# Attention with weights times values as three rounded products, row maxima from 64 rows, and reciprocals in four pieces

## The chip, the cores and the metric

The kernel runs as one program on 1 core of one Trainium2 chip. The metric is the device time of an execution in microseconds (us); lower is better. Matmul durations in the profile are modelled from their start, so consecutive matmul rows overlap; what a matmul costs is read from the distance between starts.

## The reference

One layer of a bidirectional encoder is applied with the same weights to two sequences, x_prompt (2048 tokens) and x_sample (256 tokens), all in float32 with a model width of 1024:

```python
h = rmsnorm(x, norm1_w)
p = h @ w_in                                    # 4*512 mLSTM columns, 32 gates, 512 q, 2*128 k and v
m_out = mlstm_mixer(mq, mk, mv, mo, gates, ...) # 8 heads of 64, both directions
a_out = attention_mixer(aq, ak, av, q_norm_w, k_norm_w)
x = x + concat([m_out, a_out]) @ w_out
h = rmsnorm(x, norm2_w)
a, g = split(centred_dwconv(h @ w_up, conv_w, conv_b))
x = x + (silu(g) * a) @ w_down                  # d_ff = 2816
y = rmsnorm(x, final_norm_w)
```

The attention part has 8 query heads and 2 key/value heads of 64 elements. For each group of four heads:

```python
s = einsum('bqhgd,bkhd->bhgqk', qi, k) * 64 ** -0.5
p = softmax(s, axis=-1)
o = einsum('bhgqk,bkhd->bqhgd', p, v)
```

q and k are RMS-normed per head and rotated by position; their norm weights are drawn 8 times larger than usual, so the scores are large and the softmax is sharp.

## The kernel before

A matmul here takes a stationary operand of at most 128 rows (the contraction) by 128 columns and streams a moving operand of at most 512 columns past it. Most products are written as three products of rounded parts: a float32 value x is split into a high part of type F32R (a copy through that type, made on ACT) and a low part x minus high (made on DVE, which writes F32R too); high*high + high*low + low*high is summed in PSUM. F32R operands go through the array in one pass of the matmul instruction. Plain F32 operands are turned into two matmul instructions each.

The program has these stages. `phase_a` projects q, k, v and the gates of every 128-token tile (18 tiles: 16 of the prompt, 2 of the sample), norms and rotates q and k, and stores the high and low parts of q and k (`q_d`, `k_d`) and v (`v_d`) in DRAM. `gate_math` works out the mLSTM gates. Then `run_both` interleaves two generators, `attention` and `mlstm`, by estimates of their cost that they yield; when mLSTM is through, `phase_c` (the product with w_out, tile `po`) follows beside what is left of attention. `phase_d` is the feed-forward part. The code is recorded in this order with priorities, and a scheduler of the tile framework then sets the order of the instructions on each engine from its own model of time. Each engine runs its list in that order.

Attention handles 36 pieces, each of 512 queries (tile names carry head and block): 32 of the prompt, with 16 key tiles of 128 keys, and 4 of the sample, with 2 key tiles. That makes 520 key tiles in all. Per piece:

- `prep` (L488 on) transposes the stored q into `qq` (rows 0 to 63 are q's high part, rows 64 to 127 its low part, 512 queries wide) and `qm` (high part alone, 65 rows; row 64 takes the negated maxima).
- `maxstep` (L512 to L517) takes 128 queries against 512 keys. The stationary operand is `qq`, all 128 rows, the moving one is `kk`, which holds the high part of k twice; DVE reduces the 512 scores of each query to a maximum. A prompt piece has 16 such steps, each one matmul `px` and one reduction `mx`. They belong to the piece after the current one.
- `prep2` (L519 on) reduces the maxima, negates them, and brings them as a row into `qm`.
- `scores` (L532 to L542), for two key tiles at a time: two matmuls per key tile into a PSUM tile `ps` (L539: k high with q high and low; L540: k low and a row of ones with q high and the row of negated maxima), then an exponential on ACT (L541) into the SBUF tile `pe`. With the maxima inside the product, `pe` is already exp(s - max).
- `values` (L544 to L552), two steps of the loop later (`PLAG` = 2): the product of `vv` and `pe` in F32, one for each key tile, added up in the PSUM tile `pv`. `vv` has 64 columns of v and 64 of ones, so rows 64 to 127 of `pv` get the sum of the weights.
- `fin1` (L554 on) copies both halves of `pv` out; `fin2` (L563 on) takes one reciprocal of 64x512 on DVE (L564), multiplies on POOL and stores by a DMA on POOL's queue.

PSUM tiles named `ps`, `px`, `pq` and `pr` share four banks (`SCB` = 4). `load_kv` loads kk, kl and vv for a group of heads in four parts by DMAs on POOL's queue.

Of the kernel before, what the change touches and what calls it, by code (L numbers as in the profile page):

```python
# [17 lines left out]
P = 128  # L18
# [52 lines left out]
PB = 4  # L71
PEB = 5
PLAG = 2
# [12 lines left out]
def f32(ap):  # L86
    return ap.bitcast(F32)
# [50 lines left out]
def phase_a(g, tc, sw, st_x, after_x, after_mm, after_pj):  # L138
# [3 lines left out]
    with ExitStack() as st:  # L142
# [284 lines left out]
def attention(g, tc, s1, s2, pp):  # L427
# [12 lines left out]
    def load_kv(grp, k0, k1, after=None):  # L440

        if (grp, k0) in kv:
            return
        n = k1 - k0
        sp = s2 if n == NT1 else s1
        kv[(grp, k0)] = parts = []
        for t0 in range(0, n, 4):
            m = min(4, n - t0)
            s = f"{n}_{t0}"
            kk = sp.tile([P, m * P], F32R, tag="kk" + s, name=f"kk{grp}_{s}", bufs=1)  # L450
            kl1 = sp.tile([65, m * P], F32R, tag="kl1" + s, name=f"kl1{grp}_{s}", bufs=1)
            vv = sp.tile([P, m, P], F32, tag="vv" + s, name=f"vv{grp}_{s}", bufs=1)
            c = slice((k0 + t0) * P, (k0 + t0 + m) * P)
            if after is not None:
                for t in (kk[0:1, 0:1], kk[HD:HD + 1, 0:1], kl1[0:1, 0:1], vv[0:1, 0, 0:1]):
                    nc.gpsimd.tensor_copy(t, after[0:1, 0:1])
            nc.gpsimd.memset(vv[:, :, HD:P], 1.0)
# [30 lines left out]
    def prep(n):  # L488
# [15 lines left out]
        nc.scalar.activation(s.qq[:, 0:s.N], f32(pq[:, 0:s.N]), AF.Copy)  # L504
        s.qm = sp.tile([65, 512], F32R, tag="qm", name="qm" + s.nm, bufs=2)
        nc.scalar.activation(s.qm[0:HD, 0:s.N], f32(pq[0:HD, 0:s.N]), AF.Copy)
        s.mx = sp.tile([P, 4, 4], F32, tag="mx", name="mx" + s.nm, bufs=2)
        s.nsp = -(-s.nk * P // 512)
        s.todo = [(t, z) for z in range(s.nsp) for t in range(s.nq)]
        return s  # L510

    def maxstep(s):  # L512
        t, z0 = s.todo.pop(0)
        w = min(512, s.nk * P - z0 * 512)
        ps = pp.tile([P, 512], F32, tag="sc", name=f"px{s.nm}_{t}_{z0}")
        nc.tensor.matmul(ps[:, 0:w], s.qq[:, t * P:(t + 1) * P], s.kv[z0][0][:, 0:w], start=True, stop=True)  # L516
        nc.vector.tensor_reduce(s.mx[:, t, z0:z0 + 1], ps[:, 0:w], AX.X, ALU.max)  # L517

# [13 lines left out]
    def scores(s, kp):  # L532
        N = s.N
        pe = sp.tile([P, 2, 512], F32, tag="pe", name=f"pe{s.nm}_{kp}", bufs=PEB)
        for z in range(2):
            ps = pp.tile([P, 512], F32, tag="sc", name=f"ps{s.nm}_{kp}_{z}")
            kk, kl1, _ = s.kv[kp // 2]
            kc = (2 * kp + z) % 4 * P
            nc.tensor.matmul(ps[:, 0:N], kk[:, kc:kc + P], s.qq[:, 0:N], start=True, stop=False)  # L539
            nc.tensor.matmul(ps[:, 0:N], kl1[:, kc:kc + P], s.qm[:, 0:N], start=False, stop=True)  # L540
            nc.scalar.activation(pe[:, z, 0:N], ps[:, 0:N], AF.Exp)  # L541
        return kp, pe  # L542

    def values(s, kp, pe):  # L544

        N = s.N
        if kp == 0:
            s.pv = pp.tile([P, 512], F32, tag="pv", name="pv" + s.nm, bufs=1)
        for z in range(2):
            kt = 2 * kp + z  # L550
            nc.tensor.matmul(s.pv[:, 0:N], s.kv[kp // 2][2][:, kt % 4, :], pe[:, z, 0:N], start=(kt == 0),  # L551
                             stop=(kt == s.nk - 1))  # L552

# [8 lines left out]
    def fin2(s):  # L562
        N = s.N  # L563
        nc.vector.reciprocal(s.rs[:, 0:N], s.rs[:, 0:N])  # L564
        nc.gpsimd.tensor_tensor(s.o1[:, 0:N], s.o1[:, 0:N], s.rs[:, 0:N], ALU.mult)
# [8 lines left out]
    while cur.todo:  # L574
        maxstep(cur)
        yield 0.5
    prep2(cur)
    load_kv(0, 0, NT1, cur.m4)
    old = None
    for n in range(len(hbs)):  # L580
# [3 lines left out]
        for kp in range(nkp):  # L584
# [3 lines left out]
            if nxt is not None and nxt.todo:  # L588
                if n == len(hbs) // 2 - 1:

                    k = 2 * (kp - 2) - (nxt.nq * nxt.nsp - len(nxt.todo))
                else:
                    k = -(-len(nxt.todo) // max(nkp - kp - MXE, 1))
# [648 lines left out]
def body(tc, aps, phases="abcd"):  # L1242
# [5 lines left out]
    with ExitStack() as st:  # L1248
# [6 lines left out]
        def dram(name, shape):  # L1255
            setattr(g, name, dp.tile(shape, F32, name=name))
# [6 lines left out]
        dram("k_d", [2, P, T])  # L1263
        dram("v_d", [2, P, NT, HD])
        dram("nm_d", [NT, 16, P])
# [157 lines left out]
```

## Time and profile before

| | us |
|---|---|
| three runs | 3505.19, 3510.44, 3514.43 |
| median of the runs | 3510.44 |
| profiled execution, span from first to last instruction | 3509.1 |
| first 270 us (phase_a): PE busy / DVE busy | 229.9 / 199.9 |
| 270 to 1812 us (attention beside mLSTM, then beside phase_c): PE / DVE / ACT busy | 1524.8 / 791.8 / 705.6 of 1542 |
| 1812 us to the end: PE / DVE busy | 1652.1 / 1354.2 of 1697.1 |

The profiled execution is listed with its span alone; it is 1.3 us below the median of the runs. The first `pv` matmul starts at 271.8 us, the last at 1812.0 us. In the profile PE is the matmul itself, PEld the loading of its stationary operand; DVE, ACT and POOL are the vector, scalar and general-purpose engines. In a row of groups, "x520 | 292.7, 595" means 520 instructions that kept the engine busy for 292.7 us together, 595 ns each in the mean; behind the second bar stands how long the engine was idle just before them and what ended that. In a row of the timeline the first number is the start in us, the second the time from the first start to the last end of the instructions merged into the row.

### The profile page before, as it was taken

Reading aid. Unit: us, or ns where it says so; the run is one execution under the profiler, and the core shown is the slowest. Engines: PE = TensorE matmul, PEld = TensorE weight load, DVE = VectorE, ACT = ScalarE, POOL = GpSimd, SP = SyncE. Lnnn points to the kernel's source line nnn. Section 1 sums busy time; section 2 is a strip of 40 time slices with the busy share of each in tenths; the row PEclk is TensorE's granted clock in tenths of the full one; section 3 lists DMA queues with packets and bytes.
Section 4 is the critical chain, followed back from the end, with each engine's and each line's share of the span. In section 5 each row is a group of like instructions: output and inputs, shape, how many; then the busy total and the mean of one; then the engine's idle time right before and its main releaser. Section 6 shows DMA issues by size and latency. Waiting matters only on the chain.

```text
span 3509.1 us, 53243 instructions
## 1 busy us (share of the span) xinstructions
PE 3406.8 (97%) x19538; PEld 3031.7 (86%) x19538; DVE 2345.9 (67%) x3962; ACT 1683.3 (48%) x3827; POOL 1144.3 (33%) x1362
## 2 busy tenths in 40 slices
PE   7889999999999999999999999999999999999998
PEld 6787787777777777767789999999999999999998
DVE  7773365546544555664444887878888879887777
ACT  5434454444444454453332544445544445655555
POOL 7863022213231322311135333224433224422222
PEclk9999999999999999999999999999999999999999
DMA  7765233233243434442247323213323213312211
GB/s 234 209 188 147 89 107 100 92 108 106 84 123 111 137 114 133 126 147 80 88 147 252 125 97 103 73 67 123 137 98 108 73 67 123 135 64 73 73 67 54
DMA packets 288917, 401.76 MB, mean 114 GB/s; under 512 B 27408, under 2 KB 188976, under 8 KB 288656
## 3 DMA queue, kind: packets, MB, share of 16 engines
q1 hardware_dynamic: 256560, 355.87, 30.9%
q0 software_dynamic: 10640, 31.86, 3.2%
q10 hardware_dynamic: 21456, 10.62, 1.0%
q8 instruction: 154, 2.52, 0.3%
q14 instruction: 107, 0.88, 0.1%
HBM read 315.55 MB, written 82.72 MB: 113 GB/s over the span
## 4 chain that ended last, share of the span: by engine, by line
PE 75%; DVE 9%; issue 5%; POOL 4%; DMA 4%; ACT 3%; SPq 0%; POOLq 0%; DVEq 0%; ACTq 0%
PE pa L1034 12%; PE pv L551 11%; PE pd L1172 11%; PE pc L1034 6%; PE po L918 5%; PE mv L668 4%; PE mj L658 4%; PE ps L539 3%; PE ps L540 3%; PE px L516 3%; PE pb L1034 3%; PE mN L794 1%; PE mj L684 1%; DVE acc L1174 1%; DVE y L1128 1%
## 5 line engine op out<-in xcount | busy, mean ns | idle before, releaser
L1172 PE MATMUL pd<-act,wd 128*128 128x384 f32 (+1 forms) x3120 | 592.0, 336 | 19.2 <-DVE acc L1174 10.8
L1172 PEld LDWEIGHTS pd<-act,wd 128*128 128x128 f32 x3120 | 540.0, 188 | 26.0 <-DVE acc L1174 14.5
L551 PE MATMUL pv<-pe,vv 128*128 128x512 f32 x1040 | 514.4, 593 | 0.2
L517 DVE TENSOR_REDUCE mx<-px 128x1 f32<-128x512 f32 (+1 forms) x528 | 342.8, 673 | 196.6 <-PE px L516 194.9
L1034 PE MATMUL pa<-nt,wut 128*128 128x386 f32 (+2 forms) x2376 | 454.7, 339 | 2.2 <-ACT u L1050 2.2
L1034 PEld LDWEIGHTS pa<-nt,wut 128*128 128x128 f32 x2376 | 422.2, 190 | 2.5 <-ACT u L1050 2.5
L541 ACT ACTIVATE pe<-ps 128x512 f32<-128x512 f32 x520 | 292.7, 595 | 266.2 <-PE ps L540 262.4
L1039 POOL TENSOR_TENSOR tw<-ru 128x512 f32<-128x512 f32 x66 | 102.1, 1547 | 740.3 <-DMA ru<-w_up 598.6
L1128 DVE SCALAR_TENSOR_TENSOR y<-u,cw,y 128x768 f32<-128x768 f32 (+1 forms) x264 | 308.9, 1171 | 35.8 <-ACT y L1121 28.8
L1174 DVE TENSOR_TENSOR acc<-pd,acc 128x384 f32<-128x384 f32 (+1 forms) x544 | 281.5, 538 | 40.1 <-PE pd L1172 38.1
L1050 ACT ACTIVATE u<-pa 128x386 f32<-128x386 f32 (+2 forms) x264 | 128.8, 488 | 328.3 <-PE pa L1034 325.8
L551 PEld LDWEIGHTS pv<-pe,vv 128*128 128x128 f32 x1040 | 189.0, 189 | 82.8 <-issue 58.3
L539 PE MATMUL ps<-qq,kk 128*128 128x512 f32 x520 | 249.5, 483 | 0.9 <-ACT pe L541 0.6
L918 PE MATMUL po<-cmx,wo 128*128 128x256 f32 x1728 | 242.5, 291 | 1.6 <-DVE wo L107 1.6
L918 PEld LDWEIGHTS po<-cmx,wo 128*128 128x128 f32 x1728 | 222.3, 191 | 24.7 <-issue 17.1
L516 PE MATMUL px<-kk,qq 128*128 128x512 f32 (+1 forms) x528 | 224.5, 455 | 2.7 <-ACT pe L541 1.3
L658 PE MATMUL mj<-mn,wm 128*128 128x256 f32 x1296 | 213.2, 305 | 8.6 <-ACT og L672 4.6
L658 PEld LDWEIGHTS mj<-mn,wm 128*128 128x128 f32 x1296 | 181.8, 194 | 38.0 <-issue 21.1
L540 PE MATMUL ps<-qm,kl 65*128 65x512 f32 x520 | 207.4, 402 | 0.1
L668 PE MATMUL mv<-wm,mn 128*128 128x256 f32 x1296 | 205.0, 298 | 0.4 <-ACT qb L664 0.4
L668 PEld LDWEIGHTS mv<-wm,mn 128*128 128x128 f32 x1296 | 178.1, 192 | 21.6 <-issue 13.9
L226 PE MATMUL pj<-w_a,n1T 128*128 128x512 f32 (+1 forms) x864 | 180.2, 363 | 8.6 <-DVE n1T L184 6.0
(285 smaller groups left out, 6663.8 us busy)
## 6 DMA issues: line engine op xcount, KB each, us to landing
ru<-w_up SPq DMA_DIRECT2D x132, 512.0 KB, 3.2
mn<-n_d SPq DMA_DIRECT2D x216, 256.0 KB, 3.3
rd<-w_down SPq DMA_DIRECT2D x66, 512.0 KB, 3.3
n_d<-n1T SPq DMA_DIRECT2D x18, 1024.0 KB, 5.2
dm<-nm_d POOLq DMA_DIRECT2D x72, 256.0 KB, 3.6
mjn<-n_d SPq DMA_DIRECT2D x72, 256.0 KB, 2.9
mvn<-n_d SPq DMA_DIRECT2D x72, 256.0 KB, 3.2
q_d<-qz SPq DMA_DIRECT2D x18, 512.0 KB, 5.6
```

The source lines that it names most:

```text
L516: nc.tensor.matmul(ps[:, 0:w], s.qq[:, t * P:(t + 1) * P], s.kv[z0][0][:, 0:w], start=True, stop=True)
L517: nc.vector.tensor_reduce(s.mx[:, t, z0:z0 + 1], ps[:, 0:w], AX.X, ALU.max)
L539: nc.tensor.matmul(ps[:, 0:N], kk[:, kc:kc + P], s.qq[:, 0:N], start=True, stop=False)
L540: nc.tensor.matmul(ps[:, 0:N], kl1[:, kc:kc + P], s.qm[:, 0:N], start=False, stop=True)
L551: nc.tensor.matmul(s.pv[:, 0:N], s.kv[kp // 2][2][:, kt % 4, :], pe[:, z, 0:N], start=(kt == 0), stop=(kt == s.nk - 1))
L658: nc.tensor.matmul(pj[:, o], s.w[c][:, a, o * P:(o + 1) * P], nT[c][:, h, :], start=(c + o + k == 0), stop=(c == NCC - 1 and k == 2 and o ...
L668: nc.tensor.matmul(pv[:, o], nT[c][:, a, o * P:(o + 1) * P], s.w[c][:, h, 256:512], start=(c + o + k == 0), stop=(c == NCC - 1 and k == 2 ...
L918: nc.tensor.matmul(po[:, o], wo[c][z // 2][:, a, n], mx[c][:, h, :], start=(c == 0 and k == 0), stop=(c == NCC - 1 and k == 2))
L1034: nc.tensor.matmul(p, w[:, aa, c, :], ops[k][:, c, bb, 0:n], start=c == 0 and i == 0 and not add, stop=c == NCC // 2 - 1 and i == 2, skip_ ...
L1128: nc.vector.scalar_tensor_tensor(y[:, s:e], u[:, s + k:e + k], cw[:, k, jj:jj + 1], y[:, s:e], ALU.mult, ALU.add)
L1172: nc.tensor.matmul(po, wds[j][c // 4][:, aa, c % 4 * P:(c % 4 + 1) * P], acts[j][:, bb, z0:z1], start=(j == 0 and k == 0), stop=(j == len( ...
L1174: nc.vector.tensor_tensor(accs[c][:, z0:z1], po, accs[c][:, z0:z1], ALU.add)
```

## The change

- **Values.** After the exponential, ACT copies `pe` to F32R (high part) and DVE subtracts it from `pe` (low part); both go into an SBUF tile `xx`. `phase_a` splits v in the same way and stores both parts; `load_kv` loads v's high part into `vv` (now F32R) and its low part into a new tile `vl` with 64 columns. For each key tile there are three F32R products into `pv`: vv with the high part, vl with the high part (only rows 0 to 63 of `pv`), vv with the low part.
- **Maxima.** `maxstep` takes q's high part alone: stationary operands of 64 rows, one half of the queries from rows 0 to 63 of `qm`, the other from rows 64 to 127, where `prep` now puts a second copy of q's high part. Two steps are issued together, one in each half of the rows, into two PSUM tiles; then the two reductions. The maxima are those of k high times q high.
- **Reciprocals.** The reciprocal of 64x512 becomes four of 64x128.
- `PEB` goes from 5 tiles of 2x512 to 3 of 512; `XB` = 6 tiles of 2x512 hold the two parts.

```diff
-PEB = 5
+PEB = 3
+XB = 6
...
         def post1(i, pj):
...
-            v = sp.tile([P, 2, HD], F32, tag="v", name=f"v{i}", bufs=2)
-            nc.scalar.activation(v, pj[:, 640:768].rearrange("p (h d) -> p h d", d=HD), AF.Copy)
-            nc.scalar.dma_start(g.v_d[:, :, i, :].rearrange("g p d -> p g d"), v)
+            v = sp.tile([P, 2, 2, HD], F32R, tag="v", name=f"v{i}", bufs=2)
+            pv = pj[:, 640:768].rearrange("p (h d) -> p h d", d=HD)
+            nc.scalar.activation(v[:, :, 0], pv, AF.Copy)
+            nc.vector.tensor_tensor(v[:, :, 1], pv, f32(v[:, :, 0]), ALU.subtract)
+            nc.scalar.dma_start(g.v_d[:, :, i].rearrange("g p a d -> p g a d"), f32(v))
...
-            vv = sp.tile([P, m, P], F32, tag="vv" + s, name=f"vv{grp}_{s}", bufs=1)
+            vv = sp.tile([P, m, P], F32R, tag="vv" + s, name=f"vv{grp}_{s}", bufs=1)
+            vl = sp.tile([P, m, HD], F32R, tag="vl" + s, name=f"vl{grp}_{s}", bufs=1)
...
-            nc.gpsimd.dma_start(vv[:, :, 0:HD], g.v_d[grp, :, k0 + t0:k0 + t0 + m])
-            parts.append((kk, kl1, vv))
+            for a, t in ((0, vv[:, :, 0:HD]), (1, vl)):
+                nc.gpsimd.dma_start(f32(t), g.v_d[grp, :, k0 + t0:k0 + t0 + m, a])
+            parts.append((kk, kl1, vv, vl))
...
-        s.qm = sp.tile([65, 512], F32R, tag="qm", name="qm" + s.nm, bufs=2)
-        nc.scalar.activation(s.qm[0:HD, 0:s.N], f32(pq[0:HD, 0:s.N]), AF.Copy)
+        s.qm = sp.tile([P, 512], F32R, tag="qm", name="qm" + s.nm, bufs=2)
+        for r in (0, HD):
+            nc.scalar.activation(s.qm[r:r + HD, 0:s.N], f32(pq[0:HD, 0:s.N]), AF.Copy)
...
-        s.todo = [(t, z) for z in range(s.nsp) for t in range(s.nq)]
+        s.todo = [(t, z) for z in range(s.nsp) for t in range(0, s.nq, 2)]
...
-        ps = pp.tile([P, 512], F32, tag="sc", name=f"px{s.nm}_{t}_{z0}")
-        nc.tensor.matmul(ps[:, 0:w], s.qq[:, t * P:(t + 1) * P], s.kv[z0][0][:, 0:w], start=True, stop=True)
-        nc.vector.tensor_reduce(s.mx[:, t, z0:z0 + 1], ps[:, 0:w], AX.X, ALU.max)
+        pxs = [pp.tile([P, 512], F32, tag="sc", name=f"px{s.nm}_{t0 + i}_{z0}") for i in range(2)]
+        for i in range(2):
+            r, c = slice(HD * i, HD * i + HD), slice((t0 + i) * P, (t0 + i + 1) * P)
+            nc.tensor.matmul(pxs[i][:, 0:w], s.qm[r, c], s.kv[z0][0][r, 0:w], start=True, stop=True)
+        for i in range(2):
+            nc.vector.tensor_reduce(s.mx[:, t0 + i, z0:z0 + 1], pxs[i][:, 0:w], AX.X, ALU.max)
...
-            nc.tensor.matmul(ps[:, 0:N], kl1[:, kc:kc + P], s.qm[:, 0:N], start=False, stop=True)
-            nc.scalar.activation(pe[:, z, 0:N], ps[:, 0:N], AF.Exp)
+            nc.tensor.matmul(ps[:, 0:N], kl1[:, kc:kc + P], s.qm[0:HD + 1, 0:N], start=False, stop=True)
+            pe = sp.tile([P, 512], F32, tag="pe", name=f"pe{s.nm}_{kp}_{z}", bufs=PEB)
+            x = sp.tile([P, 2, 512], F32R, tag="px", name=f"xx{s.nm}_{kp}_{z}", bufs=XB)
+            nc.scalar.activation(pe[:, 0:N], ps[:, 0:N], AF.Exp)
+            nc.scalar.activation(x[:, 0, 0:N], pe[:, 0:N], AF.Copy)
+            nc.vector.tensor_tensor(x[:, 1, 0:N], pe[:, 0:N], f32(x[:, 0, 0:N]), ALU.subtract)
...
-        for z in range(2):
+        vv, vl = s.kv[kp // 2][2:4]
+        for z, x in enumerate(xs):
             kt = 2 * kp + z
-            nc.tensor.matmul(s.pv[:, 0:N], s.kv[kp // 2][2][:, kt % 4, :], pe[:, z, 0:N], start=(kt == 0),
-                             stop=(kt == s.nk - 1))
+            nc.tensor.matmul(s.pv[:, 0:N], vv[:, kt % 4, :], x[:, 0, 0:N], start=kt == 0, stop=False)
+            nc.tensor.matmul(s.pv[0:HD, 0:N], vl[:, kt % 4, :], x[:, 0, 0:N], start=False, stop=False)
+            nc.tensor.matmul(s.pv[:, 0:N], vv[:, kt % 4, :], x[:, 1, 0:N], start=False, stop=kt == s.nk - 1)
...
-        nc.vector.reciprocal(s.rs[:, 0:N], s.rs[:, 0:N])
+        for t in range(s.nq):
+            c = slice(t * P, (t + 1) * P)
+            nc.vector.reciprocal(s.rs[:, c], s.rs[:, c])
```

The scheduler takes the two maxima matmuls of a step apart in most cases. On PE, before, in a prompt piece of head 4 beside the mLSTM projection `mv` (px is a maxima matmul, ps scores, pv values; 128x512 is the result):

```order
L668 MATMUL mv_0_5189<-wm_6_4792,mn_0_6_5124 128x256 x2
L516 MATMUL px_4_0_1_4711<-kk_16_4_2657,qq_4_4676 128x512
L668 MATMUL mv_0_5189<-wm_6_4792,mn_0_6_5124 128x256 x3
L516 MATMUL px_4_1_1_4714<-kk_16_4_2657,qq_4_4676 128x512
L551 MATMUL pv_4_4894<-pe_4_1_4702,vv_16_0_2646 128x512
L794 MATMUL mN_3_5306<-va_1_2478,dm_3_5051 128x65 x4
L776 MATMUL mS_4_5327<-qb_2_2480,mkT_2_2479 128x256
L516 MATMUL px_4_2_1_4717<-kk_16_4_2657,qq_4_4676 128x512
```

On PE after the change, in a piece of the same head beside the projection `mj` (L524 is the maxima matmul now, with 64 rows; L566, L567 and L568 are the three value products):

```order
L568 MATMUL pv_4_5920<-xx_4_7_0_6289,vv_16_12_2715 128x512
L524 MATMUL px_4_0_0_6352<-kk_16_0_2665,qm_4_6332 128x512
L676 MATMUL mj_3_6872<-mn_3_3_6859,wm_3_5232 128x256 x4
L524 MATMUL px_4_1_0_6353<-kk_16_0_2665,qm_4_6332 128x512
L676 MATMUL mj_3_6872<-mn_3_3_6859,wm_3_5232 128x256
L676 MATMUL mj_3_6872<-mn_3_4_6860,wm_4_5233 128x256
L524 MATMUL px_4_2_0_6358<-kk_16_0_2665,qm_4_6332 128x512
L676 MATMUL mj_3_6872<-mn_3_4_6860,wm_4_5233 128x256 x4
L566 MATMUL pv_4_5920<-xx_4_7_1_6297,vv_16_12_2715 128x512
L755 MATMUL mu_3_7164<-va_1_5292,kw_3_6573 128x130
L567 MATMUL pv_4_5920<-xx_4_7_1_6297,vl_16_12_2716 64x512
```

In both, maxima matmuls stand singly between full-height matmuls; the 64-row ones now do so with another height than their neighbours. Over the whole program the 528 maxima matmuls of the changed kernel stand in 414 stretches without another matmul between: 327 of one, 65 of two, 17 of three and 5 of four. The 520 matmuls L567 stand singly.

On DVE the same stage before, with the reductions `mx` between the mLSTM's operations:

```order
L517 TENSOR_REDUCE mx_4_4680<-px_4_0_1_4711 128x1
L517 TENSOR_REDUCE mx_4_4680<-px_4_1_1_4714 128x1
L795 TENSOR_TENSOR s_3_5102<-mN_3_5306,s_3_5102 128x260
L779 TENSOR_TENSOR dm_4_5104<-dm_4_5104,mS_4_5327 128x256 x2
L797 SCALAR_TENSOR_TENSOR dn_3_5312<-s_3_5102 128x4
L517 TENSOR_REDUCE mx_4_4680<-px_4_2_1_4717 128x1
```

And after, with the subtraction L554 that makes the low part of the weights, and the reciprocals L582:

```order
L526 TENSOR_REDUCE mx_4_5805<-px_4_0_0_5822 128x1
L828 SCALAR_TENSOR_TENSOR hh_6_6408<-ogr_6_6036,hh_6_6408 128x128
L554 TENSOR_TENSOR xx_4_0_1_5818<-pe_4_0_1_5817,xx_4_0_1_5818 128x512
L526 TENSOR_REDUCE mx_4_5805<-px_4_1_0_5823 128x1
L526 TENSOR_REDUCE mx_4_5805<-px_4_2_0_5828 128x1
L582 RECIPROCAL rs_4_5790<-rs_4_5790 64x128 x4
L526 TENSOR_REDUCE mx_4_5805<-px_4_3_0_5829 128x1
L554 TENSOR_TENSOR xx_4_1_0_5880<-pe_4_1_0_5879,xx_4_1_0_5880 128x512
```

DVE has one more instruction for each key tile in this stage. Of the 36 pieces, 26 have their four reciprocals directly one behind the other.

More of the change, by code (lines that the diff above doesn't have):

```diff
@@ L451, in load_kv @@
             kl1 = sp.tile([65, m * P], F32R, tag="kl1" + s, name=f"kl1{grp}_{s}", bufs=1)
[L452 removed]
+            vv = sp.tile([P, m, P], F32R, tag="vv" + s, name=f"vv{grp}_{s}", bufs=1)
+            vl = sp.tile([P, m, HD], F32R, tag="vl" + s, name=f"vl{grp}_{s}", bufs=1)
             c = slice((k0 + t0) * P, (k0 + t0 + m) * P)
             if after is not None:
[L455 removed]
+                for t in (kk[0:1, 0:1], kk[HD:HD + 1, 0:1], kl1[0:1, 0:1], vv[0:1, 0, 0:1], vl[0:1, 0, 0:1]):
                     nc.gpsimd.tensor_copy(t, after[0:1, 0:1])
[L457 removed]
+            nc.gpsimd.memset(f32(vv[:, :, HD:P]), 1.0)
             for r in (0, HD):
@@ L533, in scores, with values @@
         N = s.N
-        pe = sp.tile([P, 2, 512], F32, tag="pe", name=f"pe{s.nm}_{kp}", bufs=PEB)
+        xs = []
+        kk, kl1 = s.kv[kp // 2][0:2]
         for z in range(2):
             ps = pp.tile([P, 512], F32, tag="sc", name=f"ps{s.nm}_{kp}_{z}")
-            kk, kl1, _ = s.kv[kp // 2]
             kc = (2 * kp + z) % 4 * P
             nc.tensor.matmul(ps[:, 0:N], kk[:, kc:kc + P], s.qq[:, 0:N], start=True, stop=False)
[L540 to L544, printed above, removed]
+            nc.tensor.matmul(ps[:, 0:N], kl1[:, kc:kc + P], s.qm[0:HD + 1, 0:N], start=False, stop=True)
[4 more added lines that the diff above has]
+            nc.vector.tensor_tensor(x[:, 1, 0:N], pe[:, 0:N], f32(x[:, 0, 0:N]), ALU.subtract)
+            xs.append(x)
+        return kp, xs
+    def values(s, kp, xs):
         N = s.N
```

8 lines of the change are left out of this document (4 added, 4 removed).

## The prediction

> **What bounds the kernel now.** I read first the table of stretches (busy time of each engine), cut at the first and last values matmul:
>
> ```profile
> core 0: us, PE busy (x) PEld busy (x) DVE busy (x) ACT busy (x) POOL busy (x), PEclk, DMA share, GB/s
> 0.00:270.00 270.00, 229.90 (x1311) 200.03 (x1312) 199.92 (x339) 122.75 (x204) 200.21 (x277) 0.95 0.71 212
> 270.00:1812.00 1542.00, 1524.76 (x8520) 1190.12 (x8519) 791.83 (x1718) 705.57 (x1932) 358.41 (x680) 1.00 0.35 110
> ```
>
> Nearly all of the change lies in the 1542 us of the second row. There PE is idle for 1542 - 1524.8 = 17 us, at the full clock (1.00), while DVE is busy for 51% and ACT for 46%. So PE's instruction stream sets the time of this stage: what is taken from it or put into it counts in full, and work on DVE and ACT counts only where it makes PE wait.
>
> Then the groups of instructions that the change touches:
>
> ```profile
> L551 PE MATMUL pv<-pe,vv 128*128 128x512 f32 x1040 | 514.4, 593 | 0.2
> L516 PE MATMUL px<-kk,qq 128*128 128x512 f32 x512 | 219.8, 459 | 2.6 <-ACT pe L541 1.3 <-DVE mx L517 1.1
> L517 DVE TENSOR_REDUCE mx<-px 128x1 f32<-128x512 f32 x512 | 336.8, 682 | 187.1 <-PE px L516 185.4
> L564 DVE RECIPROCAL rs<-rs 64x512 f32<-64x512 f32 x36 | 120.2, 3340 | 87.8 <-ACT rs L560 87.6
> L541 ACT ACTIVATE pe<-ps 128x512 f32<-128x512 f32 x520 | 292.7, 595 | 266.2 <-PE ps L540 262.4
> ```
>
> The 520 F32 products of the values are 1040 matmuls. Matmul durations overlap (459 ns here), so prices have to come from distances between starts.
>
> **Values on PE: the gain.** The timeline of single instructions, PE first, then weight loads (PEld):
>
> ```profile
> 1207.37 0.40 PE L540 MATMUL ps<-qm,kl 65*128 65x512 f32 x1
> 1207.61 0.40 PE L539 MATMUL ps<-qq,kk 128*128 128x512 f32 x1
> 1207.84 0.40 PE L540 MATMUL ps<-qm,kl 65*128 65x512 f32 x1
> 1208.08 0.39 PE L516 MATMUL px<-kk,qq 128*128 128x512 f32 x1
> ```
> ```profile
> 1212.42 0.19 PEld L551 LDWEIGHTS pv<-pe,vv 128*128 128x128 f32 x1
> 1212.85 0.19 PEld L551 LDWEIGHTS pv<-pe,vv 128*128 128x128 f32 x1 [0.24 <-issue]
> 1213.28 0.19 PEld L551 LDWEIGHTS pv<-pe,vv 128*128 128x128 f32 x1 [0.24 <-issue]
> 1213.71 0.19 PEld L684 LDWEIGHTS mj<-mjn,wm 128*128 128x128 f32 x1 [0.24 <-issue]
> ```
>
> Three F32R matmuls of 512 columns follow one another in 0.71 us, 0.235 us each. The F32 ones are 0.43 us apart, and there are two for each key tile: 0.86 us. Three F32R products cost 3 x 0.235 = 0.705 us. The gain is 520 x 0.155 = 81 us. The 64-column `vl` product streams 512 columns like the others, so I give it the same price.
>
> Whether that product costs something for its narrow shape can be read in phase_a, where a transposition with 40 columns (L290) stands between 128-column matmuls:
>
> ```profile
> 153.89 0.63 PE L226 MATMUL pj<-w_a,n1T 128*128 128x512 f32 x2
> 154.36 0.38 PE L290 MATMUL pg<-ident,gp 128*40 128x128 f32 x2
> 154.49 0.48 PE L226 MATMUL pj<-w_a,n1T 128*128 128x512 f32 x1
> ```
> ```profile
> 154.13 0.33 PEld L290 LDWEIGHTS pg<-ident,gp 128*40 128x40 f32 x2
> 154.47 0.30 PEld L226 LDWEIGHTS pj<-w_a,n1T 128*128 128x128 f32 x2
> ```
>
> The two L226 matmuls end at 154.52, yet the weights of L290 load from 154.13, while the last of them streams, and L226's from 154.47, before L290 ends. Going to fewer columns and back waits for nothing.
>
> **Maxima on PE: the loss.** A matmul with at most 64 rows is the other new shape. Before, it occurs only in gate_math, as a transposition of 40 rows (L378) between the projections:
>
> ```profile
> 248.12 0.19 PEld L658 LDWEIGHTS mj<-mn,wm 128*128 128x128 f32 x1
> 248.44 0.13 PEld L378 LDWEIGHTS gpt<-ident,rows 40*128 40x128 f32 x1
> 248.94 0.30 PEld L658 LDWEIGHTS mj<-mn,wm 128*128 128x128 f32 x2
> 252.70 0.30 PEld L668 LDWEIGHTS mv<-wm,mn 128*128 128x128 f32 x2
> ```
> ```profile
> 247.88 0.64 PE L658 MATMUL mj<-mn,wm 128*128 128x256 f32 x4
> 248.44 0.25 PE L378 MATMUL gpt<-ident,rows 40*128 40x40 f32 x1
> 248.59 0.42 PE L378 MATMUL gpt<-ident,rows 40*128 40x40 f32 x4
> 248.94 0.39 PE L658 MATMUL mj<-mn,wm 128*128 128x256 f32 x1
> 252.36 0.42 PE L378 MATMUL gpt<-ident,rows 40*128 40x40 f32 x4
> 252.71 0.39 PE L668 MATMUL mv<-wm,mn 128*128 128x256 f32 x1
> ```
> ```profile
> 250.96 0.28 PE L658 MATMUL mj<-mn,wm 128*128 128x256 f32 x1
> ```
> ```profile
> L378 PE MATMUL gpt<-ident,rows x18: 229/230/251, 248.4 to 252.5; 40*128 40x40 f32 x18
> ```
>
> L658 ends at 247.88 + 0.64 = 248.52, and the weights of L378 load at 248.44, 0.08 us before that end. L378 ends at 249.01 (second place: 252.78), and the next full-height weights load at 248.94 (252.70), again 0.07 to 0.08 before the end. At no such border is a weight load drawn forward as at L290; it begins when the matmul before it has almost run out. Besides, the first full matmul behind it takes 0.39 us where one between its like takes 0.28 (row at 250.96): it waits 0.11 for its weights.
>
> For a 512-column matmul, which lasts 0.395 but gives way after 0.235, a border then costs 0.395 - 0.07 - 0.235 = 0.09 us of running out and 0.11 us of bare weight load, 0.20 us. Each stretch of 64-row matmuls has two borders, 0.40 us. The order on PE shows 414 stretches: 414 x 0.40 = 166 us. Bounds: from below, the load on entry may be nearly covered (L378's first matmul takes 0.25 against a median of 0.23, 0.02 exposed): 0.09 + 0.02 + 0.20 = 0.31 us, 128 us; if the rows describe only transpositions, 0. From above 166: a load of 65 rows lasts as long as one of 128.
>
> ```profile
> 1207.61 0.19 PEld L540 LDWEIGHTS ps<-qm,kl 65*128 65x128 f32 x1
> ```
>
> I take 166, because F32R weights load in 0.19 us here like L658's, and not in 0.13 like L378's.
>
> The Trainium skill says the same for this border: "Mode switching requires drain: Changing tiling mode (not just tile) drains the TensorE" (TensorEngine Tiling (Array Packing), Key Properties). This case's trace agrees at L378, whose loads start 0.08 us before the end ahead of them, and disagrees at L290, whose load starts 0.39 us before it.
>
> What the two halves can save: within a stretch, 64-row matmuls of different halves may run side by side. Stretches of two, three and four hold 65 + 17 + 5 x 2 = 92 pairs, at most 92 x 0.235 = 22 us; if they don't overlap, 0. No row shows two halves at once; I take the middle, 11 us.
>
> **ACT and DVE: hidden, with a little loss.** Per key tile a copy on ACT and a subtraction on DVE are new, for which the nearest rows are the same operations on the same shape in phase_d:
>
> ```profile
> L1030 ACT ACTIVATE wut<-ru 128x512 fp32r<-128x512 f32 x132 | 82.2, 623 | 29.7 <-PE pb L1034 25.5 <-PE pc L1034 2.0 <-POOL ru L1041 1.9
> L1031 DVE TENSOR_TENSOR wut<-ru,wut 128x512 fp32r<-128x512 f32 x132 | 103.0, 780 | 42.3 <-ACT wut L1030 41.9 <-issue 0.3
> L506 ACT ACTIVATE qm<-pq 64x512 fp32r<-64x512 f32 x36 | 20.8, 578 | 0.0
> ```
>
> ACT gets 520 x 0.623 = 324 us and 36 x 0.578 = 21 us for the second copy of q: 706 + 345 = 1051. DVE gets 520 x 0.78 = 406 us: 792 + 406 = 1198. Four reciprocals of a quarter each take 36 x 3.34 = 120 us as before if time goes with columns, and are mostly adjacent in DVE's order, so they let nothing else through; I count 0. The reductions stay as they are. Against a stage of some 1610 us DVE is busy for 74% and ACT for 65%. The path from scores to values grows from the exponential (0.595) to 0.595 + 0.623 + 0.78 = 2.0 us, but a values product stands two loop steps behind its scores, and 260 steps in 1542 us make 5.9 us each; PE has other matmuls there. This is the cover; if it goes, each of the 260 steps waits up to 1.4 us. PE's idle time may rise from 17 us to perhaps 50, or fall, as each PE step is longer: bounds -15 and +35; I take +5, near the row of now.
>
> Small terms: in phase_a 18 subtractions of 128x128 from PSUM, where PE is idle for 40 of 270 us; and ten more DMA issues on POOL's queue for v's low part, behind which the next part's loads wait. Their nearest rows:
>
> ```profile
> L267 DVE TENSOR_TENSOR kz<-t,kz 128x128 fp32r<-128x128 f32 x18 | 7.5, 417 | 0.0
> ```
> ```profile
> 1206.88 0.61 POOL L755 DMA_DIRECT2D dm<-nm_d  x1 [3.81 <-PE px L516]
> ```
>
> The first is 18 x 0.417 = 7.5 us of DVE, 0 to 8 us on the path; I take 3. The second is 10 x 0.61 = 6 us of POOL, which is busy for 23% of the stage; I take 1.
>
> **Sum.** -81 + 166 - 11 + 5 + 3 + 1 = +83 us on the profiled 3509.1 us, 3592 us. The span is 1.3 us under the median of the runs; on the median it is 3593. Own range: -81 + 128 - 22 - 15 + 0 = +10 (3520) to -81 + 166 + 35 + 9 = +129 (3639), some more for what the order does at the borders.
>
> **Rivals.**
>
> (a) The 64-row border is free for F32R matmuls, and what L378 shows belongs to transpositions. For it: only 18 matmuls and three borders are quoted. Against: transpositions with full height or 40 columns wait for nothing (L290). Then -81 - 22 + 5 + 4 = -94: 3417 us.
>
> (b) The border to fewer columns makes the array run out as well. `vl` stands singly 520 times, so at the 0.40 us of a 64-row stretch this adds 208 us: 3801. For it: L290 is a transposition, `vl` an F32R product. Against: L290 waits for nothing. At 0.08 us a border it eats the whole gain of 81 us (520 x 2 x 0.08). The sentence quoted from the Trainium skill (TensorEngine Tiling (Array Packing), Key Properties) speaks of every change of mode and so for this rival; the trace disagrees at L290.
>
> (c) DVE becomes the bound. For it: in the first row of the table DVE reaches 199.9 of 270 us, 74%, and there PE already idles for 40 us. If 74% is all that dependencies allow, 1198 us of DVE need 1619 us, which the forecast's stage fills anyhow; if only 70%, 1711 us, 169 more than now: 3680. It decides when PE's rows grow idle before L566 and L524 with DVE as the releaser. Against: in phase_d DVE runs at 1354 of 1697 us (80%) beside a PE that is busy for 97%.
>
> ```profile
> 1812.00:3509.10 1697.10, 1652.10 (x9712) 1641.50 (x9710) 1354.15 (x1905) 854.97 (x1693) 585.67 (x406) 0.99 0.30 103
> ```
>
> **How the numbers follow.** Forecast 0.68 (3520 to 3650, likeliest 3593); rival (a) 0.20; (b) 0.04; (c) 0.05; something between (a) and the forecast, within 0.3% of before, 0.03. A difference of 0.3% (about 10 us) is what a measurement of this kernel can tell. Faster: (a) and a few low ends, 0.21. Same: 0.05. Slower: the rest, 0.74. For 8 in 10 the range must take in part of (a): 3412 to 3655.
>
> **What would show it.** Right: L524 starts about 0.32 us after the matmul before it began, the full matmul behind it shows a first duration of about 0.5 instead of 0.39 us, values cost 0.70 us a key tile, PE stays busy for over 97% of the stage, and the stage ends some 80 us later. Wrong: L524 follows at 0.235 us (then (a)); L567 has the same gaps (b); PE idle before L566 or L524 by tens of us, ended by DVE (c). Most of all the forecast would fail if two borders cost less than 0.2 us together, as 81 us then outweigh them.

## The result and the profile after

| | median of the runs, us | profiled span, us |
|---|---|---|
| before | 3510.93 (3505.19 to 3514.43, 4 runs) | 3509.1 |
| with the change | 3610.08 (3603.08 to 3613.01, 4 runs) | 3601.4 |

The ratio is 1.0282, with a 95% interval from 1.0268 to 1.0297: the change makes the kernel slower by 2.8%. The forecast was 3593 us, with a range of its own from 3520 to 3650; the range for 8 in 10 went from 3412 to 3655.

The table of stretches of the profile after, cut at its first and last values matmul (for the kernel before, the cut at the same events stood at 270 and 1812 us):

```profile
core 0: us, PE busy (x) PEld busy (x) DVE busy (x) ACT busy (x) POOL busy (x), PEclk, DMA share, GB/s
0.00:277.90 277.90, 235.34 (x1350) 204.58 (x1351) 209.62 (x365) 128.88 (x217) 213.49 (x290) 0.95 0.73 218
277.90:1895.20 1617.30, 1586.17 (x8984) 1247.65 (x8983) 1116.79 (x2334) 996.74 (x2474) 388.18 (x680) 0.99 0.33 104
1895.20:3601.30 1706.10, 1657.27 (x9730) 1646.35 (x9728) 1366.09 (x1909) 855.90 (x1694) 581.86 (x406) 0.99 0.30 103
```

The stage of attention grew from 1542 to 1617 us. PE is idle in it for 31 us instead of 17, so it still is PE's stream that sets the time: 61 of the 75 us are busy time of PE. DVE and ACT rose to 69% and 62% of the stage. The rest of the 92 us lies ahead of this stretch (8 us, 2 of them because the cut of before stands 1.9 us ahead of its first values matmul) and behind it (9 us, where 18 more matmuls stand behind the cut).

The groups that answer to those shown of before:

```profile
L524 PE MATMUL px<-kk,qm 64*128 64x512 f32 x512 | 207.6, 493 | 2.7 <-ACT pe L552 1.1 <-ACT qm L512 1.0 <-DVE mx L526 0.2
L568 PE MATMUL pv<-xx,vv 128*128 128x512 f32 x520 | 218.9, 421 | 8.7 <-DVE xx L554 8.6
L554 DVE TENSOR_TENSOR xx<-pe,xx 128x512 fp32r<-128x512 f32 x520 | 367.7, 719 | 206.1 <-ACT xx L553 202.5 <-PE mv L686 2.5
L582 DVE RECIPROCAL rs<-rs 64x128 f32<-64x128 f32 x144 | 122.5, 902 | 23.2 <-ACT rs L576 23.1
```

The values products now do wait for DVE, 8.6 us in all for the third of them. What the maxima cost can't be read from their group; the timeline shows it. A single 64-row matmul between full-height ones, PE and then the weight loads:

```profile
291.43 0.40 PE L676 MATMUL mj<-mn,wm 128*128 128x256 f32 x2
291.66 0.39 PE L755 MATMUL mu<-va,kw 128*128 128x130 f32 x2
291.98 0.49 PE L524 MATMUL px<-kk,qm 64*128 64x512 f32 x1
292.40 0.51 PE L676 MATMUL mj<-mn,wm 128*128 128x256 f32 x2
```
```profile
291.55 0.30 PEld L755 LDWEIGHTS mu<-va,kw 128*128 128x128 f32 x2
291.98 0.18 PEld L524 LDWEIGHTS px<-kk,qm 64*128 64x128 f32 x1
292.40 0.30 PEld L676 LDWEIGHTS mj<-mn,wm 128*128 128x128 f32 x2 [0.24 <-issue]
```

L755 ends at 291.66 + 0.39 = 292.05, and the 64-row weights load only from 291.98. L524 lasts 0.49 instead of 0.39 us, since it waits for these weights, and ends at 292.47; the full-height weights load from 292.40. The two L676 behind it take 0.51 where two of them otherwise take 0.40 (row at 291.43). These are the two borders: from the start of L524 to the next start it is 0.42 instead of 0.235 us (0.185), the next matmul gives way 0.11 later, and the one before it 0.09 later (the second L755 starts 0.39 - 0.28 = 0.11 after the first, at 291.77, and L524 only 0.21 after that). Together 0.39 us, as forecast (0.40).

The narrow product with `vl` behind the one with `vv`:

```profile
284.53 0.50 PE L566 MATMUL pv<-xx,vv 128*128 128x512 f32 x1
284.87 0.40 PE L567 MATMUL pv<-xx,vl 128*64 128x512 f32 x1
```
```profile
284.63 0.14 PEld L567 LDWEIGHTS pv<-xx,vl 128*64 128x64 f32 x1
```

Its weights load at 284.63, long before L566 ends at 285.03, and it lasts 0.40 us as any other: no border there.

Where PE does wait for DVE, the order of DVE's own list is behind it. This is the longest of the ten waits at L568: ACT's copy, DVE's instructions, then PE.

```profile
826.42 0.63 ACT L553 ACTIVATE xx<-pe 128x512 fp32r<-128x512 f32 x1
```
```profile
826.55 1.28 DVE L526 TENSOR_REDUCE mx<-px 128x1 f32<-128x512 f32 x2
827.75 0.28 DVE L766 SCALAR_TENSOR_TENSOR C<-C,dec,C 128x65 f32<-128x65 f32 x1
827.94 1.28 DVE L526 TENSOR_REDUCE mx<-px 128x1 f32<-128x512 f32 x2
829.14 0.68 DVE L554 TENSOR_TENSOR xx<-pe,xx 128x512 fp32r<-128x512 f32 x1
```
```profile
827.62 0.40 PE L567 MATMUL pv<-xx,vl 128*64 128x512 f32 x1
829.88 0.53 PE L568 MATMUL pv<-xx,vv 128*128 128x512 f32 x1 [1.86 <-DVE xx L554]
```

The copy is through at 827.05, but four reductions for the next piece's maxima and an mLSTM operation stand ahead of the subtraction in DVE's list, and it starts at 829.14. It takes 0.68 us, as most do (the median of the 520 is 0.684). At all ten waits one of the two instructions directly ahead of the subtraction is a reduction L526. An order with the subtractions ahead of the reductions was not tried.

Such a wait may cost more than its own length. Behind this one the granted clock (PEclk, the share of its full rate that PE was given) falls from 1.00 to 0.50 for 10 us:

```profile
823.00:830.20 7.20, 5.18 (x21) 2.61 (x18) 6.48 (x16) 2.34 (x4) 0.00 (x0) 1.00 0.00 0
830.25:840.40 10.15, 10.08 (x32) 8.44 (x32) 6.66 (x19) 6.36 (x12) 0.56 (x1) 0.50 0.07 22
```
```profile
833.63 0.63 PE L549 MATMUL ps<-qm,kl 65*128 65x512 f32 x1
834.06 0.63 PE L548 MATMUL ps<-qq,kk 128*128 128x512 f32 x1
```

In it the matmuls of 512 columns follow 0.43 instead of 0.235 us apart. The stage has five stretches at half clock, 31 us together; before it had three, 10 us together. In each of the eight PE had been idle for at least 1.0 us within the 3.4 us before. By these lengths half the clock takes about 15 us of this stage and took 5 before, an estimate. That the waits bring the clock down fits all eight, but no run tests it by itself.

### The profile page after: what moved, and what is told of

The parts are those of the page before. It is cut to its first block, busy times and chain, and to the rows that moved or that the text cites. A ratio compares the mean times of both kernels' runs of the same rounds, so it can differ in the third digit from the quotient of the medians.

```text
span 3601.4 us, 55931 instructions
## 1 busy us (share of the span) xinstructions
PE 3478.8 (97%) x20058; PEld 3098.6 (86%) x20058; DVE 2692.5 (75%) x4608; ACT 1981.5 (55%) x4383; POOL 1183.5 (33%) x1376
## 5 line engine op out<-in xcount | busy, mean ns | idle before, releaser
L554 DVE TENSOR_TENSOR xx<-pe,xx 128x512 fp32r<-128x512 f32 x520 | 367.7, 719 | 206.1 <-ACT xx L553 202.5
L526 DVE TENSOR_REDUCE mx<-px 128x1 f32<-128x512 f32 (+1 forms) x528 | 345.1, 672 | 104.8 <-PE px L524 102.5
L553 ACT ACTIVATE xx<-pe 128x512 fp32r<-128x512 f32 x520 | 317.2, 631 | 5.2
L568 PE MATMUL pv<-xx,vv 128*128 128x512 f32 x520 | 218.9, 421 | 8.7 <-DVE xx L554 8.6
L686 PE MATMUL mv<-wm,mn 128*128 128x256 f32 x1296 | 216.9, 295 | 1.8 <-ACT qb L682 1.8
L548 PE MATMUL ps<-qq,kk 128*128 128x512 f32 x520 | 215.3, 417 | 3.1 <-ACT pe L552 2.6
L566 PE MATMUL pv<-xx,vv 128*128 128x512 f32 x520 | 215.4, 414 | 2.5 <-ACT xx L553 1.6
L686 PEld LDWEIGHTS mv<-wm,mn 128*128 128x128 f32 x1296 | 185.5, 193 | 35.9 <-issue 19.2
L524 PE MATMUL px<-kk,qm 64*128 64x512 f32 (+1 forms) x528 | 212.7, 489 | 3.1 <-ACT qm L512 1.2
L676 PEld LDWEIGHTS mj<-mn,wm 128*128 128x128 f32 x1296 | 179.3, 190 | 39.6 <-issue 17.6
L676 PE MATMUL mj<-mn,wm 128*128 128x256 f32 x1296 | 206.3, 291 | 6.3 <-ACT og L690 4.7
```

What stands on the lines that cost most here:

```text
L526: nc.vector.tensor_reduce(s.mx[:, t0 + i, z0:z0 + 1], pxs[i][:, 0:w], AX.X, ALU.max)
L553: nc.scalar.activation(x[:, 0, 0:N], pe[:, 0:N], AF.Copy)
L554: nc.vector.tensor_tensor(x[:, 1, 0:N], pe[:, 0:N], f32(x[:, 0, 0:N]), ALU.subtract)
L568: nc.tensor.matmul(s.pv[:, 0:N], vv[:, kt % 4, :], x[:, 1, 0:N], start=False, stop=kt == s.nk - 1)
L676: nc.tensor.matmul(pj[:, o], s.w[c][:, a, o * P:(o + 1) * P], nT[c][:, h, :], start=(c + o + k == 0), stop=(c == NCC - 1 and k == 2 and o ...
L686: nc.tensor.matmul(pv[:, o], nT[c][:, a, o * P:(o + 1) * P], s.w[c][:, h, 256:512], start=(c + o + k == 0), stop=(c == NCC - 1 and k == 2 ...
```

## The experiments

The theory is that of the forecast: the three products save PE time, and each stretch of 64-row matmuls costs PE 0.40 us at its borders. The rivals are that ACT and DVE make PE wait, and that the 64-column product has borders too. In the tables, "before" is the median of the kernel before, measured on the same chip together with the runs of that row.

### Each part of the change alone

Values alone: the change, with `maxstep`, `qm` and the reciprocal as before.

```diff
-            nc.tensor.matmul(pxs[i][:, 0:w], s.qm[r, c], s.kv[z0][0][r, 0:w], start=True, stop=True)
+        nc.tensor.matmul(ps[:, 0:w], s.qq[:, t * P:(t + 1) * P], s.kv[z0][0][:, 0:w], start=True, stop=True)
```

> The values in three rounded products alone; maxima with 128 rows and the undivided reciprocal as before. Border theory (each stretch of 64-row matmuls costs two borders of 0.20 us): nothing is left but the gain of 81 us on PE and small losses of about 15, 3510 - 66 = 3445, 3430 to 3470, faster than before. Rival (the loss comes from the added copies and subtractions on ACT and DVE, which make PE wait): the loss stays, 3590 to 3620. Rival (borders of the 64-column product): 3600 and more.

Maxima alone: the kernel before with the new `maxstep` and `qm`.

```diff
-        nc.tensor.matmul(ps[:, 0:w], s.qq[:, t * P:(t + 1) * P], s.kv[z0][0][:, 0:w], start=True, stop=True)
+            nc.tensor.matmul(pxs[i][:, 0:w], s.qm[r, c], s.kv[z0][0][r, 0:w], start=True, stop=True)
```

> The maxima from 64 rows alone; values in F32 and the undivided reciprocal as before. Its order has 423 stretches of 64-row matmuls, with 87 pairs side by side. Border theory: 423 x 0.40 - 87 x 0.235 = +149, about 3660 (3630 to 3680). Rival (ACT and DVE): about as before or up to 20 us faster, 3490 to 3515, since nothing but a small copy is added there.

Reciprocals alone: the kernel before with the four pieces.

```diff
-        nc.vector.reciprocal(s.rs[:, 0:N], s.rs[:, 0:N])
+        for t in range(s.nq):
+            c = slice(t * P, (t + 1) * P)
+            nc.vector.reciprocal(s.rs[:, c], s.rs[:, c])
```

> The reciprocals in four pieces alone. DVE has time, and the pieces mostly stand together: 3510, within 0.3% of before, by either theory. The pieces should take 0.84 us each if time goes with the columns.

| part alone | median, us | before, us | ratio (95% interval) |
|---|---|---|---|
| values | 3462.43 | 3509.92 | 0.9859 (0.9841 to 0.9876) |
| maxima | 3643.56 | 3509.92 | 1.0382 (1.0367 to 1.0397) |
| reciprocals | 3506.08 | 3509.92 | 0.999 (0.9981 to 0.9999) |

The values save 47 us and the maxima cost 134. This settles the main question: the loss comes with the maxima, where ACT and DVE have next to nothing new to do, and without the 64-row matmuls the change is a gain. In the stage with the maxima alone PE is idle for 9 us only, so these 134 us are PE's own time:

```profile
270.20:1944.60 1674.40, 1665.48 (x8529) 1182.78 (x8529) 802.58 (x1723) 729.14 (x1969) 359.58 (x677) 1.00 0.33 101
```

The price of 423 stretches was put at 149 us; 134 were measured, partly since waits of PE shrank from 17 to 9 us. Over the whole execution PE is busy for 138 us more (3545.1 instead of 3406.8); with the 80 pairs that start together in this trace (80 x 0.235 = 19 us) that makes some 0.37 us a stretch. The values alone came out at the upper end of what was expected. Their stage, from the first to the last values matmul:

```profile
273.30:1746.70 1473.40, 1443.14 (x8933) 1247.66 (x8932) 1113.04 (x2228) 973.84 (x2439) 385.02 (x680) 0.99 0.36 113
```

It lost 69 us of 1542: PE is busy for 82 us less and idle for 13 us more. The 82 us are not the products alone, since 107 other matmuls of before fall outside this stretch (8933 instead of 8520 + 520). Over the whole execution PE is busy for 76 us less (3331.1 instead of 3406.8), near the 81 us of the products, and idle for 17 us more. This profiled execution gains 59 us, where the median gains 47: it is the fastest of four, at a granted clock of 0.990, and the other three had 0.986 to 0.988. The four reciprocals take 0.90 us each (0.84 expected) and change nothing that matters.

The three parts add up to -47 + 134 - 4 = +83 us, and together they cost 99. In the profiled executions the gap is 21 us (+71 against +92). Of these, 12 us are waits of PE, which is idle for 20 us more than before where the parts give 8, and 9 us are busy time, 72 us more than before where the parts give 63. The granted clock of the whole execution is 0.986 with the change, and 0.990, 0.990 and 0.989 with the parts; 0.004 of 3601 us is 14 us. So what the parts don't have, the change has in PE's waits and in stretches at half clock; why it waits more often than the parts isn't settled.

### The two halves side by side

The change, with both matmuls of a step on rows 0 to 63.

```diff
-            r, c = slice(HD * i, HD * i + HD), slice((t0 + i) * P, (t0 + i + 1) * P)
+            r, c = slice(0, HD), slice((t0 + i) * P, (t0 + i + 1) * P)
```

> The change, but both maxima matmuls of a step take rows 0 to 63, so that no two can run side by side; 409 stretches instead of 414. If the halves do overlap (92 pairs, 0.235 us each), this costs 22 us more than the change, about 3632 (3622 to 3642); if they don't, it stays at 3610 (3600 to 3615).

Measured: 3607.16 us, ratio 1.0274 (1.0255 to 1.0293), not to be told from the change itself. By the time alone, then, the halves would not overlap. Yet the traces show that they do run side by side. Two of them with the change, in different halves:

```profile
876.25 0.40 PE L676 MATMUL mj<-mn,wm 128*128 128x256 f32 x2
876.59 0.49 PE L524 MATMUL px<-kk,qm 64*128 64x512 f32 x2
877.01 0.51 PE L676 MATMUL mj<-mn,wm 128*128 128x256 f32 x2
```

Both take 0.49 us together, as the single one did above, and the next matmul starts 0.42 us after them, as behind one. With both on the same rows, three of them take 0.96 us:

```profile
383.38 0.96 PE L524 MATMUL px<-kk,qm 64*128 64x512 f32 x3
384.27 0.50 PE L566 MATMUL pv<-xx,vv 128*128 128x512 f32 x1
```

PE's busy time in L524 grows accordingly:

```profile
L524 PE MATMUL px<-kk,qm 64*128 64x512 f32 x512 | 227.4, 479 | 2.4 <-ACT qm L512 2.0
```

That is 20 us more than with the change (207.6), close to the 22 us of 92 pairs (85 of them start together in the trace of the change, which makes 20). The total doesn't show it: in the stage PE's idle time is 23 us instead of 31, and the waits for DVE fall from 8.6 to 5.3 us at L568, so part of it went into time in which PE would have waited. The rest can't be told from the spread of the runs (3597.96 to 3614.29) and the slightly different order.

### The pairs kept together

The change, with `px` and `ps` in tiles of two banks, two of them instead of four banks, so that both matmuls of a step wait for one tile.

```diff
-        pxs = [pp.tile([P, 512], F32, tag="sc", name=f"px{s.nm}_{t0 + i}_{z0}") for i in range(2)]
+        px = pp.tile([P, 2, 512], F32, tag="sc", name=f"px{s.nm}_{t0}_{z0}")
+        pxs = [px[:, i] for i in range(2)]
...
-SCB = 4
+SCB = 2
```

> The change, but the four PSUM banks become two tiles of two banks, so that both maxima matmuls of a step wait for the same tile and stand together: 251 stretches instead of 414, with 259 pairs instead of 92. Border theory: 163 stretches fewer at 0.40 us, 65 us, and 167 pairs more side by side at 0.23 us, 38 us: 3610 - 103 = 3507 (3490 to 3570, as two banks now come free together and scores may wait). If borders were not the cause, it would stay at 3610 or grow by the waits for banks.

Measured: 3642.01 us, ratio 1.0376 (1.0361 to 1.0392): slower than the change, 135 us above the expected value. Its stage:

```profile
275.70:1970.40 1694.70, 1603.63 (x9251) 1261.79 (x9249) 1138.96 (x2376) 1023.11 (x2493) 389.66 (x684) 0.95 0.34 104
```

PE is idle for 91 us instead of 31, and the granted clock fell to 0.95: 164 us of this stage ran at half clock, in 22 stretches, instead of 31 us in five. Who waited for whom, in this kernel (us in total, times, longest):

```profile
PEld pv L570 <- DVE xx L556: 56.6, 65, 3.3
PE pv L570 <- DVE xx L556: 32.5, 29, 2.6
...
PEld ps L550 <- ACT pe L554: 28.7, 69, 1.3
...
PEld px L525 <- ACT pe L554: 22.1, 32, 2.0
```

With the change the four rows stood at 14.9, 8.6, 4.3 and 8.1 us. Scores and maxima now wait until ACT has both exponentials out of a tile, and the values come late in turn. So the time of this run doesn't isolate the borders. PE's work does show them: over the whole execution PE is busy for 20 us less than with the change (3458.9 instead of 3478.8), although more of it ran at half clock. With the busy time at half clock counted half, it is about 74 us less (3362 instead of 3436, an estimate from the two traces), of the 103 us expected. Against that stand 59 us more of PE's waits and some 54 us by the clock: banks which come free in twos cost more here than 163 stretches fewer bring. How the change would fare with its pairs together and its banks single wasn't tried.

### What bounds the values alone

Without the product of v's low part, which is left out here:

```diff
-            nc.tensor.matmul(s.pv[0:HD, 0:N], vl[:, kt % 4, :], x[:, 0, 0:N], start=False, stop=False)
```

> The values alone (128-row maxima, undivided reciprocal), without the product of v's low part, which is left out: two F32R products for each key tile. If PE's stream sets the time, 520 x 0.235 = 122 us less than the run with the values alone: 3462 - 122 = 3340 (3335 to 3365). If ACT and DVE already bound this stage, hardly less than 3462.

With a product of full width in its place:

```diff
-            nc.tensor.matmul(s.pv[0:HD, 0:N], vl[:, kt % 4, :], x[:, 0, 0:N], start=False, stop=False)
+            nc.tensor.matmul(s.pv[:, 0:N], vv[:, kt % 4, :], x[:, 0, 0:N], start=False, stop=False)
```

> The values alone, with vv in the place of vl in the second product: 128 columns and all rows of the output instead of 64; v's low part is left out by this, and the high part counts twice. If borders to 64 columns cost nothing, the same as the run with the values alone, 3462 (3450 to 3475). If each cost 0.05 us or more, 52 us less or more, below 3410.

Without the subtraction on DVE:

```diff
-            nc.vector.tensor_tensor(x[:, 1, 0:N], pe[:, 0:N], f32(x[:, 0, 0:N]), ALU.subtract)
...
-            nc.tensor.matmul(s.pv[:, 0:N], vv[:, kt % 4, :], x[:, 1, 0:N], start=False, stop=kt == s.nk - 1)
+            nc.tensor.matmul(s.pv[:, 0:N], vv[:, kt % 4, :], x[:, 0, 0:N], start=False, stop=kt == s.nk - 1)
```

> The values alone, without the subtraction on DVE: the third product takes the high part again, so PE does the same work and the low part of the weights is left out. DVE loses 373 us in the stage. By the account of the trace (PE idle for 30 us there with the values alone, 17 before) it gains what those waits cost, 10 to 20 us: 3440 to 3455. If DVE were close to being the bound, it would gain 40 us and more.

| values alone, and | median, us | before, us | ratio (95% interval) |
|---|---|---|---|
| nothing else | 3462.43 | 3509.92 | 0.9859 (0.9841 to 0.9876) |
| no product of v's low part | 3381.32 | 3510.86 | 0.9633 (0.9618 to 0.9647) |
| that product with 128 columns | 3463.36 | 3510.86 | 0.9869 (0.9853 to 0.9886) |
| no subtraction | 3435.67 | 3510.86 | 0.9788 (0.9773 to 0.9804) |

The width of the second product makes no difference: the rival of the 64-column borders has fallen, on the trace and on the time. The subtraction costs (0.9859 - 0.9788) x 3510 = 25 us, above the 10 to 20 expected and below the 40 of a DVE that is close to being the bound; by the two intervals it is between some 17 and 33 us. Between the two profiled executions, the fastest of the one kernel and the slowest of the other, it is 10 us only, and PE's idle time in the stage is 19 us instead of 30. With the values alone not only the products wait for the subtraction: the exponential waits for it 17.8 us in all, until one of the three `pe` tiles (`PEB` = 3) is free. More tiles were not tried, and no run leaves out the copy on ACT. A product less saves 81 us (79 by the ratios) instead of 122. Two thirds of the price of a product come through. PE is then idle for 52 us of the stage, and the granted clock of the whole execution is 0.983 instead of 0.990:

```profile
277.00:1705.90 1428.90, 1376.98 (x8730) 1218.34 (x8728) 1116.32 (x2266) 973.61 (x2458) 398.90 (x685) 0.99 0.40 123
```

So with the values in three products PE's stream still sets most of the time, but DVE, busy for 76% of the stage with the values alone and 78% in this run, has come near enough that its order tells.

### A version that beats both

Since DVE's subtraction costs 25 us, POOL can take some of them: the values alone, with every fourth or every second subtraction on POOL.

```diff
-            nc.vector.tensor_tensor(x[:, 1, 0:N], pe[:, 0:N], f32(x[:, 0, 0:N]), ALU.subtract)
+            (nc.gpsimd if z and kp % 2 else nc.vector).tensor_tensor(x[:, 1, 0:N], pe[:, 0:N], f32(x[:, 0, 0:N]), ALU.subtract)
```

> The values alone, with every fourth subtraction on POOL instead of DVE. Without any subtraction DVE's 373 us fell away and 27 us were gained; a quarter of them, 93 us, would give 7 us by the same rate: 3455 (3448 to 3462). If POOL's slower subtraction (about 1.5 us by its other operations on 128x512) is later than the values product wants it, or slows DVE, no gain or a loss: 3462 to 3480.

```diff
+            (nc.gpsimd if z else nc.vector).tensor_tensor(x[:, 1, 0:N], pe[:, 0:N], f32(x[:, 0, 0:N]), ALU.subtract)
```

> The values alone, with every second subtraction on POOL. By the rate of the run without subtractions 187 us less on DVE give 13 us: 3449 (3440 to 3458). If POOL is late or slows DVE, more so than with a quarter: 3465 to 3500.

Every fourth: 3444.25 us, ratio 0.981 (0.9797 to 0.9824), the fastest of the kernels that leave no term out. It gains 18 us on the values alone, where 7 were expected (3448 to 3462); the waits for DVE at the third product fall from 7.5 to 4.8 us, which is not enough to account for it, and the rest stays open. Every second: 3478.03 us, ratio 0.9905 (0.9891 to 0.9919), in the range expected for the case that POOL is late or slows DVE (3465 to 3500). The subtractions of the run with every second one on POOL, and the product that takes them:

```profile
L550 POOL TENSOR_TENSOR xx<-pe,xx 128x512 fp32r<-128x512 f32 x260 | 351.1, 1351 | 361.3 <-ACT xx L549 329.0 <-PE px L521 8.6 <-PE ps L545 5.9
L550 DVE TENSOR_TENSOR xx<-pe,xx 128x512 fp32r<-128x512 f32 x260 | 223.5, 860 | 195.3 <-ACT xx L549 194.8
L564 PE MATMUL pv<-xx,vv 128*128 128x512 f32 x520 | 215.9, 415 | 17.4 <-DVE xx L550 16.6 <-POOL xx L550 0.6
```

It isn't POOL that comes late (0.6 us), but DVE (16.6, against 7.5 with the values alone and 4.8 with every fourth on POOL). DVE's own subtraction takes 0.86 us in the mean, where it takes 0.73 with none on POOL and 0.78 with a quarter. The medians hardly differ (0.692, 0.685 and 0.691 us); some take far longer, up to 3.0, 1.8 and 2.7 us. In these three traces no subtraction on DVE that ran with no POOL instruction beside it, DMA issues apart, took more than 0.70 us, and all 130 of more than 0.9 us (54, 34 and 42) ran beside one. So the slow subtractions on DVE come with work on POOL. They don't account for all of the waits: at the two longest, 4.3 and 3.7 us of the 16.6, the subtraction took 0.67 and 0.68 us and stood behind reductions in DVE's order.

## Why the prediction was right

- **What bounds the stage.** Right: PE's idle time went from 17 to 31 us while its busy time grew by 61 us. That the full clock of before (1.00) would last was taken for granted, and did not quite hold (0.99).
- **Values, -81 us.** The term is right on PE: with the values alone PE is busy for 76 us less over the whole execution. The total gains only 47 us; see ACT and DVE below.
- **Narrow product, no border.** Right, read off L290 in phase_a, a transposition: the trace after shows it at L567, and the run with 128 columns takes the same time. The sentence of the Trainium skill (TensorEngine Tiling (Array Packing), Key Properties), that a change of tiling mode drains the array, agrees with these traces at the matmuls of 64 rows; at those of 64 columns they show no drain, and whether these change the mode at all no run here shows.
- **Borders, +166 us.** The mechanism is right, and so is the price of a stretch: 0.39 measured at one place and some 0.37 in the mean, against 0.40, worked out from three places with a matmul of another kind. It shows in the total as 134 us for 423 stretches (149 expected with the pairs), since some of it fell on time in which PE had waited.
- **Halves side by side, -11 us.** They do overlap, nearly in full (20 us of PE's time in L524), but in the total it can't be seen.
- **ACT and DVE, +5 us.** This is the term that was mis-sized. PE's idle time rose by 14 us in the stage and by 20 in the whole execution, and stretches at half clock, which the sum has no term for, account for some 14 us of PE's busy time. With the values alone, leaving out the subtraction gains 25 us. The cover that was named, two loop steps or some 12 us between scores and values, holds for most products, not for all. The subtraction took 0.72 us, less than the 0.78 assumed, so it isn't the price of the work that was wrong: what the forecast lacks is that DVE takes a subtraction only behind the reductions that stand ahead of it in its order.
- **Reciprocals, 0.** Right within what can be told (ratio 0.999): the pieces stand together, at 0.90 us each.
- **The small terms** were not measured by themselves. With the values alone, which has both, the first values matmul starts 1.5 us later than before (273.4 instead of 271.9 us).

The signs came as they were named: behind a matmul of 512 columns L524 starts 0.33 us after it (the median of 111 places), the full matmul of 512 columns behind L524 lasts 0.50 us, PE is busy for 98% of the stage, and the stage ends 83 us later.

The total of +83 us stands against +92 in the profiled execution and +99 in the medians. That it comes so near is luck in part. With the busy time at half clock counted half, PE's work grew by about 58 us (3378 to 3436, an estimate) where the forecast had -81 + 166 - 11 = 74; the waits and the clock took 20 + 14 us where it had 5, and 4 for the small terms. The rivals: (a) fell at the timeline after (borders at L524) and at the maxima alone; (b) at L567 and the run with full width; (c) was not the case, as PE's idle time stayed at 2% of the stage, but a small part of it, DVE's late subtractions, is what the sum lacked.

## What to carry to other kernels

A matmul with half the rows is not half a matmul where it stands between full ones: here each change of height made the array run out and load its weights bare, 0.2 us each way, and a scheduler that pulls pairs apart multiplies that. Before such shapes are used, count in the instruction order how many stretches they will stand in, and look in the trace for any place where a matmul of that shape already stands. When a kernel has one engine as its bound, work that is moved to the others isn't free because they are half idle: 373 us of subtractions on an engine at 76% cost 25 us. Look in that engine's order for what stands ahead of the work that the bound waits for, and for a lower clock behind its waits.

## What the runs showed of the hardware

Four things stand out. Two 64-row matmuls in different halves of the rows start together and cost as much as one (0.42 us to the next start for both). With two PSUM tiles of two banks instead of four of one, PE's waits grew from 31 to 91 us, and the granted clock of the stage sank from 0.99 to 0.95. The clock was either full or half: each of the 8 stretches at half clock in this stage, before and after, came behind at least 1.0 us of idle PE within 3.4 us, and in it matmuls of 512 columns were 0.43 instead of 0.235 us apart. And DVE's subtraction of 128x512 went from 0.73 to 0.78 and 0.86 us in the mean as a quarter and a half of the subtractions went to POOL; it never took more than 0.70 us with no POOL instruction other than a DMA issue beside it.
